# Second feed-forward product by seven products, a second summed buffer, and the order of the last two attention heads

## The chip, the core and the metric

The kernel runs on one core of a Trainium2 chip. A core has a matrix engine (TensorE, PE in the rows), VectorE (DVE), ScalarE (ACT), GpSimd (POOL) and SyncE (SP), which here only starts loads; the instructions of each engine run in the order in which they stand in the program, and engines wait for each other through semaphores. Matmuls read SBUF and add up in PSUM, which has eight banks of 128 x 512 float32. The metric is the device time of one execution in microseconds.

## The reference

One layer over 256 tokens of 2048 features, batch 1. What the change touches:

```
h = rms_norm(x, ffn1_norm);   x = x + 0.5 * swiglu_ffn(h, ffn1_w_in, ffn1_w_out)   # inner width 5632
h = rms_norm(x, mix_norm);    p = h @ w_mix_in            # conv value | conv gate | gMLP u | gMLP v
...                                                        # two mixers, w_mix_out
q = rms_norm(x) @ w_q;  k, v = split(rms_norm(mem) @ w_kv)   # 4 heads of 512, 256 memory tokens
p = softmax(q k^T * 512 ** -0.5);   x = x + (p v) @ w_o
x = x + 0.5 * swiglu_ffn(rms_norm(x, ffn2_norm), ffn2_w_in, ffn2_w_out);   final rms_norm
swiglu_ffn(h, w_in, w_out) = (silu(gate) * up) @ w_out,   gate | up = h @ w_in
```

## The kernel before

**Products.** Every float32 operand is held as two reduced-precision parts, high and low. A weight tile of 128 x 1024 is loaded by SP into a `raw` buffer, ACT casts its high part into an `hl` buffer (1024 columns), DVE subtracts to get the low part, and PE runs three matmuls for each product: high x high, high x low, low x high. One matmul has 128 x 512 outputs.

**First product of a feed-forward (class `FeedForward`).** The 11 groups j write the tiles `h0` to `h10` (128 x 2 x 512, tokens by features). From group 1 on a pair of k tiles is either a plain step (`eight`, 24 matmuls) or a step by seven products instead of eight (`seven`, 21 matmuls), as `PATTERNS` says; the seven products take sums of weight halves, made on DVE, and sums of input halves (`forms`), made once. For three k tiles of each group (`SUMMED`) the low part is not made by DVE: ACT writes minus the high part and the high part, and a load that adds, started by POOL, brings the low part (`summed`). The first feed-forward has two buffers for this from group 1 on (`hl_s` and half of `more`), the second has one (`hl_s`).

**Second product of the first feed-forward.** Four calls of `gemm_n`, one for each 512 output columns: 22 steps of two k tiles, 12 matmuls each (a loaded weight tile holds two k tiles of 512 columns). Its left operand is h turned by PE transposes: 22 turns, each four 128 x 128 transposes of `h` into a bank of the pool `pa` (two banks, tile `aux`), a cast by ACT and a subtraction by DVE into `hA`, `hB`, `hC` or the end of `hl_s`. Four turns stand in the last group of the first product, the other 18 in the first `gemm_n`, one for each step of 12 matmuls. The outputs `o` are copied by ACT, turned in the same way, and joined to x (`joins`), which also writes the left operand `x_hl` of the mixer's products.

**Attention.** For each head: queries, `probabilities` (scores and softmax), `turned` (four transposes of the probabilities into `p_hl`, split of the values into `v_hl`), `attend` (product with the values). For the last two heads the first k tiles of the output product `w_o` are placed between these (`begun`).

**What sets the order.** The code is recorded by a tile framework, whose scheduler orders each engine's instructions; a buffer of a pool is reused when its readers are done.

Of the kernel before, what the change touches and what calls it, by code (L numbers as in the profile page):

```python
# [11 lines left out]
F32 = mybir.dt.float32  # L12
# [5 lines left out]
P = 128  # L18
# [20 lines left out]
SUMMED = ((2, 7, 13), (2, 7, 13))  # L39

# [29 lines left out]
def layer(ctx: ExitStack, tc: tile.TileContext, a: dict):  # L70
# [108 lines left out]
    def gemm_n(w, x_hl, per=0.0, between=None, after=4):  # L179

        acc = [ps.tile([P, 2, 256], F32, name="acc").rearrange("p a b -> p (a b)") for _ in range(2)]
        nk = w.shape[1]
        for k0 in range(0, nk, 2):
# [9 lines left out]
            if between and k0 >= after:  # L193
                between.pop(0)()
# [134 lines left out]
    class FeedForward:  # L329
# [6 lines left out]
        def __init__(self, stack, tags, x_hl, gain, w_in, pattern, summed):  # L336
# [8 lines left out]
            self.h = [(low if j < 8 else high).tile([P, 2, G], F32, name=f"h{j}") for j in range(NG)]  # L345
# [19 lines left out]
            self.first = self.hls[0].rearrange("p a (f two n) -> p (a f) two n", f=2, two=2)  # L365

# [11 lines left out]
        def raw(self, j, k):  # L378
            i = self.raw_at % (4 + len(self.raws))
            self.raw_at += 1  # L380
            raw = wraw.tile([P, 1024], F32, name="raw") if i < 4 else self.raws[i - 4]
            nc.sync.dma_start(out=raw, in_=self.w_in[j, :, k])
            return raw

        def summed(self, at):
# [4 lines left out]
            raw, hl = self.raws_summed[at % len(self.hls)], self.hls[at % len(self.hls)]  # L390
# [21 lines left out]
        def x(self, k, t):  # L412
            s = slice(t * P, (t + 1) * P)
            return self.x_hl[:, k, 0, s], self.x_hl[:, k, 1, s]

        def seven(self, j, p, b, first, last):
# [8 lines left out]
            form = [(self.forms[self.spairs.index(p)][:, f, 0], self.forms[self.spairs.index(p)][:, f, 1]) for f in range(4)]  # L425
            three(b["5"], form[0], w[:, 0, lo], w[:, 1, lo], first, last)
            three(b["7"], form[2], w[:, 0, hi], w[:, 1, hi], first, last)
            nc.vector.tensor_tensor(out=one[:, lo], in0=sums[:, lo], in1=two[:, hi], op=ALU.add)
            w = self.parts(one)
            three(b["6"], form[1], w[:, 0, lo], w[:, 1, lo], first, last)  # L430
            three(b["1"], self.x(k, 0), w[:, 0, hi], w[:, 1, hi], first, last)
            w = self.parts(two)
            three(b["2"], self.x(k + 1, 0), w[:, 0, lo], w[:, 1, lo], first, False)
            three(b["3"], form[3], w[:, 0, hi], w[:, 1, hi], first, False)
            nc.vector.tensor_tensor(out=two[:, lo], in0=two[:, lo], in1=one[:, lo], op=ALU.subtract)
            w = self.parts(two, G)
            three(b["4"], self.x(k + 1, 1), w[:, 0, lo], w[:, 1, lo], first, False)
# [5 lines left out]
        def eight(self, j, p, b, first, last, plain):  # L443
            for k in (2 * p, 2 * p + 1):
                at = (j, k) in self.sums_at and self.sums_at.index((j, k))
                w = self.parts(self.raw(j, k), last=plain) if at is False else self.hls[at % len(self.hls)]
                begin = [(1, 1)] if first and k % 2 == 0 else []
                acc = [[b["2"], b["3"]], [b["4"], b["8"]]]
                by_two(acc, self.x_hl[:, k], w[:, 0], w[:, 1], k, begin, last and k % 2 == 1)
# [3 lines left out]
                self.next = None if at is False else at + len(self.hls)  # L453
# [9 lines left out]

        def group(self, j, r, after=()):
            b = {}
            for name in "57":
                b[name] = bank(ps if name == "5" else pa, "acc" if name == "5" else "aux")
            b["6"] = bank(pa, "aux")
            for name in "1234":
                b[name] = bank(ps, "acc")  # L470
            b["8"] = bank(ps, "acc")
# [3 lines left out]
            for p, c in enumerate(self.pattern):  # L475
                if c == "S":
                    self.seven(j, p, b, p == 0, p == self.spairs[-1])
# [730 lines left out]
```

## Time and profile before

| | us |
|---|---|
| median of 3 runs (lowest, highest) | 2100.37 (2097.94, 2103.01) |
| the profiled execution | 2096.62 |
| its span, first to last instruction | 2094.9 |
| PE busy | 2082.5 |
| DVE busy | 1577.4 |
| ACT busy | 1165.2 |

The table is read so: the span is the time of the profiled execution from its first instruction to its last, 1.7 us less than its device time. Busy PE is not PE at its peak, because matmuls overlap: a matmul of 512 columns is listed with 0.39 us, and the next starts 0.23 us later. So a wait of PE is seen in the distance of two starts, and a wait under about 0.16 us does not show as idle time.

### The profile page before, as it was taken

Reading aid. Unit: us, or ns where it says so; the run is one execution under the profiler, and the core shown is the slowest. Engines: PE = TensorE matmul, PEld = TensorE weight load, DVE = VectorE, ACT = ScalarE, POOL = GpSimd, SP = SyncE. Lnnn points to the kernel's source line nnn. Section 1 sums busy time; section 2 is a strip of 40 time slices with the busy share of each in tenths; the row PEclk is TensorE's granted clock in tenths of the full one; section 3 lists DMA queues with packets and bytes.
Section 4 is the critical chain, followed back from the end, with each engine's and each line's share of the span. In section 5 each row is a group of like instructions: output and inputs, shape, how many; then the busy total and the mean of one; then the engine's idle time right before and its main releaser. Section 6 shows DMA issues by size and latency. Waiting matters only on the chain.

```text
span 2094.9 us, 26646 instructions
## 1 busy us (share of the span) xinstructions
PE 2082.5 (99%) x9786; PEld 1741.6 (83%) x9786; DVE 1577.4 (75%) x2217; ACT 1165.2 (56%) x1451; POOL 67.7 (3%) x83
## 2 busy tenths in 40 slices
PE   9999999999999999999999999999999999999998
PEld 7888888888888888888888898888888888888886
DVE  7888888875655589888877666778888888787754
ACT  8665666554544454445665454556665666554443
POOL 0000000000000000000000000000000000000000
PEclk9999999999999999999999999999999999999999
DMA  9787778755665666555555543576777777556664
GB/s 368 241 263 246 226 228 263 228 183 169 226 189 188 216 233 198 187 180 183 182 197 188 186 157 117 200 272 218 217 248 251 241 225 246 182 163 203 195 192 152
DMA packets 122387, 442.34 MB, mean 211 GB/s; under 512 B 13584, under 2 KB 13968, under 8 KB 121872
## 3 DMA queue, kind: packets, MB, share of 16 engines
q1 hardware_dynamic: 113040, 407.08, 57.0%
q0 software_dynamic: 8640, 32.51, 8.3%
q8 instruction: 76, 1.25, 0.2%
q10 hardware_dynamic: 576, 1.06, 0.1%
q14 instruction: 55, 0.45, 0.1%
HBM read 438.49 MB, written 2.10 MB: 210 GB/s over the span
## 4 chain that ended last, share of the span: by engine, by line
PE 96%; DMA 2%; issue 1%; ACT 1%; DVE 0%; POOL 0%; SPq 0%; DVEq 0%; ACTq 0%; POOLq 0%
PE acc L192 12%; PE acc L191 12%; PE acc L190 12%; PE acc L319 9%; PE acc L321 9%; PE acc L318 9%; PE acc L144 8%; PE acc L151 4%; PE acc L307 3%; PE acc L305 3%; PE acc L306 3%; PE aux L293 1%; PE aux L307 1%; PE aux L305 1%; PE aux L306 1%
## 5 line engine op out<-in xcount | busy, mean ns | idle before, releaser
L116 DVE TENSOR_TENSOR hl<-raw,hl 128x1024 fp32r<-128x1024 f32 (+1 forms) x402 | 488.5, 1216 | 277.3 <-ACT hl L115 276.3
L115 ACT CAST hl<-raw 128x1024 fp32r<-128x1024 f32 (+1 forms) x402 | 419.6, 1045 | 477.8 <-PE acc L192 291.0
L373 DVE TENSOR_TENSOR hl<-spare,hl 128x1024 fp32r<-128x1024 f32 (+1 forms) x128 | 146.6, 1149 | 34.0 <-ACT hl L372 31.0
L372 ACT CAST hl<-spare 128x1024 fp32r<-128x1024 f32 (+1 forms) x128 | 126.2, 994 | 69.4 <-PE acc L321 25.9
L319 PE MATMUL acc<-hl,x_hl 128*128 128x512 f32 x408 | 147.7, 391 | 0.3 <-DVE hl L124 0.2
L373 DVE TENSOR_TENSOR hl<-raw,hl 128x1024 fp32r<-128x1024 f32 (+1 forms) x107 | 120.7, 1131 | 29.7 <-ACT hl L372 28.3
L372 ACT CAST hl<-raw 128x1024 fp32r<-128x1024 f32 (+1 forms) x107 | 103.5, 979 | 69.6 <-PE acc L321 26.7
L318 PE MATMUL acc<-hl,x_hl 128*128 128x512 f32 x408 | 141.8, 390 | 0.3 <-ACT hl L123 0.3
L321 PE MATMUL acc<-hl,x_hl 128*128 128x512 f32 x408 | 126.5, 389 | 0.0
L372 ACT CAST ring<-spare 128x1024 fp32r<-128x1024 f32 (+1 forms) x81 | 80.4, 997 | 58.9 <-PE acc L321 19.0
L373 DVE TENSOR_TENSOR ring<-spare,ring 128x1024 fp32r<-128x1024 f32 (+1 forms) x81 | 93.0, 1153 | 13.9 <-ACT ring L372 12.6
L191 PE MATMUL acc<-hl,m_hl 128*128 128x512 f32 x256 | 100.3, 392 | 0.0
L191 PE MATMUL acc<-hl,x_hl 128*128 128x512 f32 x256 | 100.3, 392 | 0.0
L192 PE MATMUL acc<-hl,m_hl 128*128 128x512 f32 x256 | 100.2, 391 | 0.0
L192 PE MATMUL acc<-hl,x_hl 128*128 128x512 f32 x256 | 99.8, 390 | 0.0
L319 PE MATMUL acc<-ring,x_hl 128*128 128x512 f32 x248 | 91.4, 389 | 0.0
L190 PE MATMUL acc<-hl,m_hl 128*128 128x512 f32 x256 | 91.2, 392 | 0.0
L318 PEld LDWEIGHTS acc<-hl,x_hl 128*128 128x128 f32 x408 | 76.4, 188 | 16.6 <-ACT hl L123 0.5
L319 PEld LDWEIGHTS acc<-hl,x_hl 128*128 128x128 f32 x408 | 76.2, 188 | 16.8 <-DVE hl L373 0.8
L190 PE MATMUL acc<-hl,x_hl 128*128 128x512 f32 x256 | 90.0, 391 | 0.0
L321 PEld LDWEIGHTS acc<-hl,x_hl 128*128 128x128 f32 x408 | 76.6, 188 | 16.0
L318 PE MATMUL acc<-ring,x_hl 128*128 128x512 f32 x248 | 88.8, 389 | 0.0
(362 smaller groups left out, 4974.9 us busy)
## 6 DMA issues: line engine op xcount, KB each, us to landing
spare<-in_ffn_w_in SPq DMA_DIRECT2D x195, 512.0 KB, 7.0
raw<-in_ffn_w_out SPq DMA_DIRECT2D x176, 512.0 KB, 3.5
raw<-in_ffn_w_in SPq DMA_DIRECT2D x156, 512.0 KB, 6.4
hl_s<-in_ffn_w_in POOLq DMA_DIRECT2D x44, 512.0 KB, 8.8
raw<-in_w_mix_vg SPq DMA_DIRECT2D x32, 512.0 KB, 4.5
raw<-in_w_k SPq DMA_DIRECT2D x32, 512.0 KB, 3.6
raw<-in_w_v SPq DMA_DIRECT2D x32, 512.0 KB, 4.3
raw<-in_w_mix_out SPq DMA_DIRECT2D x32, 512.0 KB, 4.6
```

The costliest lines, as they stand in the source:

```text
L115: nc.scalar.copy(out=hl[:, 0, :size], in_=raw[:, :size])
L116: newest[0] = nc.vector.tensor_tensor(out=hl[:, 1, :size], in0=raw[:, :size], in1=hl[:, 0, :size].bitcast(F32), op=ALU.subtract)
L144: nc.tensor.matmul(acc, lhsT=hi[:, k], rhs=xs[k], start=first and k == 0, stop=last and k == kk - 1, skip_group_check=True,)
L151: nc.tensor.matmul(acc[:, 0], lhsT=lo[:, k], rhs=xs[k][:, 0], start=False, stop=last and k == kk - 1, skip_group_check=True,)
L190: nc.tensor.matmul(acc[t], lhsT=x[:, 0, s], rhs=hi[:, k], start=k0 + k == 0, stop=False)
L191: nc.tensor.matmul(acc[t], lhsT=x[:, 0, s], rhs=lo[:, k], start=False, stop=False)
L192: nc.tensor.matmul(acc[t], lhsT=x[:, 1, s], rhs=hi[:, k], start=False, stop=k0 + k == nk - 1)
L318: nc.tensor.matmul(acc[t][g], lhsT=x[:, 0, s], rhs=hi[:, cols[g]], start=(t, g) in first, stop=False)
L319: nc.tensor.matmul(acc[t][g], lhsT=x[:, 0, s], rhs=lo[:, cols[g]], start=False, stop=False)
L321: nc.tensor.matmul(acc[t][g], lhsT=x[:, 1, s], rhs=hi[:, cols[g]], start=False, stop=last)
L372: self.cast = nc.scalar.copy(out=hl[:, 0, :n], in_=raw[:, :n])
L373: newest[0] = nc.vector.tensor_tensor(out=hl[:, 1, :n], in0=raw[:, :n], in1=hl[:, 0, :n].bitcast(F32), op=ALU.subtract)
```

## The change

It does four things.

1. The second product of the first feed-forward is computed in two blocks of 1024 output columns (`out_block`) instead of four of 512. Of the 22 pairs of k tiles four (9, 12, 15 and 18) are steps by seven. The 18 turns come faster, two or three to a pair, and the turns with numbers 9, 12, 15 and 18 also make the sums of input halves (`out_sides`). Two more `raw` buffers (`raw_out0`, `raw_out1`) and the buffer of weight sums lie where `h4` to `h6` were, two more `hl` buffers and the sums in `more_out`.
2. The first product of the mixer (`w_mix_vg`) runs its first two column groups in halves: k tiles 0 to 7 of both, then 8 to 15 of both.
3. The second feed-forward gets a second summed buffer (`hl_s2`) for the groups up to 7; `h9` and `h10` take its place later, and `h8` is its `raw` buffer until group 8 writes it.
4. In attention's last two heads the first part of `w_o` tile 1 is loaded in two halves around the turn of head 2, and the turn of head 3 is recorded before, not after, four k tiles of `w_o` tile 0.

The core of the diff:

```diff
+OUT_S = (9, 12, 15, 18)
+OUT_STEPS = (
+    list(range(KF // 2)),
+    [9, 0, 1, 12, 2, 3, 15, 4, 5, 18, 6, 7, 8, 10, 11, 13, 14, 16, 17, 19, 20, 21],
+)
...
+            if pair:
+                second = high.tile([P, 2, 1024], F32R, name="hl_s2", tag="pair")
+                self.h += [high.tile([P, 2, G], F32, name="h8"), None, None]
...
+        def buffer(self, at):
+            return at % 2 if not self.pair or self.sums_at[at][0] < 8 else 0
...
+        def out_sides(self, form, tp):
+            f1, f2 = ev.tile([P, T], F32, name="tu"), ev.tile([P, T], F32, name="tg")
+            second = ev.tile([P, T], F32, name="sq")
+            nc.scalar.copy(out=second.rearrange("p (k t) -> p k t", k=2), in_=tp[:, :, P:])
...
+            nc.vector.scalar_tensor_tensor(out=f[0], in0=a21, scalar=-1.0, in1=a22, op0=ALU.mult, op1=ALU.subtract)
+            nc.vector.scalar_tensor_tensor(out=f[1], in0=f[0], scalar=-1.0, in1=a11, op0=ALU.mult, op1=ALU.subtract)
+            nc.vector.tensor_tensor(out=f[2], in0=a11, in1=a21, op=ALU.subtract)
+            nc.vector.tensor_tensor(out=f[3], in0=a12, in1=f[1], op=ALU.subtract)
...
-        for n in range(4):
-            acc = gemm_n(a["ffn1_w_out"][n], ff.of, per=0.8 if n else 0.0, between=turns, after=0 if n == 0 else 4)
...
+        def turns_first(i):
...
+            for _ in range(2 if i < 4 else 1):
+                next_turn()
+            if i == 6:
+                stack.enter_context(ff.late)
+                ff.high.close()
+                pool = rest["pool"] = stack.enter_context(tc.tile_pool(name="ffn1", bufs=1, reuse_waits="tile"))
+                ff.sums = pool.tile([P, 1024], F32, name="sums_out")
+                ff.raws += [pool.tile([P, 1024], F32, name=f"raw_out{q}") for q in range(2)]
...
+        o = ff.out_block(0, result, turns_first, next_turn)
...
             begun(0, 0, 8)
-            begun(1, 0, 8)
+            begun(1, 0, 4)
             turn_now(2)()
+            begun(1, 4, 4)
             state["p"] = probabilities(3, q_next)
             attend(2, *state["v"])
             begun(2, 0, 8)
+            turn_now(3)()
             begun(0, 8, 4)
-            turn_now(3)()
             begun(1, 8, 4)
...
-        ff = FeedForward(stack, ("S0", "S1", "S2"), x_hl, lambda k: col("ffn2_norm", k), a["ffn2_w_in"], PATTERNS[1], SUMMED[1])
+        ff = FeedForward(stack, ("S0", "S1", "S2"), x_hl, lambda k: col("ffn2_norm", k), a["ffn2_w_in"], PATTERNS[1], SUMMED[1], pair=True)
```

How instructions move at three places. In the rows, a name's number tells buffers apart, and line numbers of the changed program are some 8 to 150 higher.

**Place 1, the last turns of h in the second product.** PE before, at the second turn of `h8` and the first of `h9` (`aux` is a turn's bank, `hl` a cast weight tile):

```order
L190 MATMUL acc_3485<-hl_3854,hB_3647 128x512
L191 MATMUL acc_3484<-hl_3854,hB_3647 128x512
L191 MATMUL acc_3485<-hl_3854,hB_3647 128x512
L293 MATMUL aux_3816<-ident_81,h8_128 128x128 x4
L293 MATMUL aux_3845<-ident_81,h9_129 128x128 x4
L192 MATMUL acc_3484<-hl_3854,hB_3647 128x512
L192 MATMUL acc_3485<-hl_3854,hB_3647 128x512
```

PE now, at all turns of `h8`, `h9` and `h10`:

```order
L329 MATMUL acc_3486<-hl_3879,hA_3455 128x512
L301 MATMUL aux_3759<-ident_81,h8_128 128x128 x4
L301 MATMUL aux_3783<-ident_81,h8_128 128x128 x4
L301 MATMUL aux_3812<-ident_81,h9_129 128x128 x4
L301 MATMUL aux_3847<-ident_81,h9_129 128x128 x4
L301 MATMUL aux_3870<-ident_81,h10_130 128x128 x4
L301 MATMUL aux_3894<-ident_81,h10_130 128x128 x4
L326 MATMUL acc_3483<-hl_3909,hA_3455 128x512
```

Before, two turns stand together and 24 matmuls lie between such pairs; now six turns stand in a row, without a matmul between them. The turn before them, the second of `h7` (`aux_3723`), stands five matmuls ahead of the first row above.

ACT before, in the same stretch (L115 casts a weight tile, L123 a turn; now L392 and L131):

```order
L123 CAST hB_3647<-aux_3768 128x2x256
L123 CAST hB_3647<-aux_3792 128x2x256
L115 CAST hl_3878<-raw_3876 128x1024
L115 CAST hl_3902<-raw_3900 128x1024
L123 CAST hB_3647<-aux_3816 128x2x256
L123 CAST hC_3844<-aux_3845 128x2x256
```

ACT now, from the second turn of `h8` to the weight tile that PE multiplies next:

```order
L131 CAST hB_3626<-aux_3783 128x2x256
L131 CAST hC_3811<-aux_3812 128x2x256
L574 COPY sq_3821<-aux_3812 128x256
L131 CAST hC_3811<-aux_3847 128x2x256
L131 CAST more_out_3528<-tu_3819 128x2x128
L131 CAST more_out_3528<-tg_3820 128x2x128
L131 CAST hC_3811<-aux_3870 128x2x256
L131 CAST hC_3811<-aux_3894 128x2x256
L392 CAST hl_3909<-raw_out1_3907 128x1024
L392 CAST hl_3926<-raw_3924 128x1024
```

Before, casts of weight tiles stood between the casts of turns; now the cast of the next weight tile, `hl_3909`, stands behind the casts of all six turns, and `out_sides` (lines 574 and on) stands among them.

**Place 2, the turn of the probabilities of head 2.** PE before (`e` the probabilities, `p_hl` turned, `v_hl` the values):

```order
L151 MATMUL acc_10144<-o_hl_9122,hl_10169 128x256 x8
L969 MATMUL aux_10189<-ident_81,e_10114 128x128
L969 MATMUL aux_10194<-ident_81,e_10114 128x128
L969 MATMUL aux_10189<-ident_81,e_10135 128x128
L969 MATMUL aux_10194<-ident_81,e_10135 128x128
L129 MATMUL acc_10247<-p_hl_10188,v_hl_10199 128x256
```

PE now:

```order
L159 MATMUL acc_10212<-o_hl_9190,hl_10264 128x256 x4
L1107 MATMUL aux_10249<-ident_81,e_10182 128x128
L1107 MATMUL aux_10254<-ident_81,e_10182 128x128
L1107 MATMUL aux_10249<-ident_81,e_10203 128x128
L1107 MATMUL aux_10254<-ident_81,e_10203 128x128
L137 MATMUL acc_10320<-p_hl_10248,v_hl_10259 128x256
```

The product that reads `p_hl` stands right behind the four transposes in both; only the weight loads ahead of them are cut otherwise.

**Place 3, ACT at the end of attention.** Before, behind the last casts of head 3 (`o_hl`):

```order
L123 CAST o_hl_9122<-acc_10384 128x256
L115 CAST hl_10457<-raw_10455 128x512
L115 CAST hl_10477<-raw_10475 128x1024
L115 CAST hl_10506<-raw_10504 128x1024
L268 ACTIVATE x_hl_10415<-xT_3478,pv_82 128x256
```

ACT now:

```order
L131 CAST o_hl_9190<-acc_10457 128x256
L123 CAST hl_10530<-raw_10528 128x512
L421 ACTIVATE hl_s2_11194<-h8_11195 128x1024
L422 CAST hl_s2_11194<-h8_11195 128x1024
L123 CAST hl_10550<-raw_10548 128x1024
L123 CAST hl_10579<-raw_10577 128x1024
```

The two instructions that fill the second summed buffer now stand ahead of the cast of a `w_o` tile.

## Rows read from the trace of the kernel before

**Rows 1.** The page: busy time by engine, and the chain that ended last

```profile
PE 2082.5 (99%) x9786; PEld 1741.6 (83%) x9786; DVE 1577.4 (75%) x2217; ACT 1165.2 (56%) x1451; POOL 67.7 (3%) x83
PE 96%; DMA 2%; issue 1%; ACT 1%; DVE 0%; POOL 0%; SPq 0%; DVEq 0%; ACTq 0%; POOLq 0%
```

**Rows 2.** PE's waits: line, what it waited for, total us, times, longest

```profile
PE acc L319 <- DMA hl_s<-in_ffn_w_in: 0.9, 1, 0.9
PE acc L129 <- ACT p_hl L123: 0.6, 1, 0.6
PE acc L129 <- DVE o_hl L124: 0.3, 1, 0.3
```

**Rows 3.** Chain in order of time: start, us, matmuls of 512, 128 and 256 columns

```profile
106.86 0.91 PE acc L318 x4
...
489.66 0.87 PE aux L293 x8
...
1099.60 1.91 PE acc L151 x16
```

**Rows 4.** Busy time by engine: second product of the first feed-forward, groups of the second

```profile
448.00:690.00 242.00, 242.00 (x1124) 200.57 (x1124) 141.88 (x167) 121.21 (x158) 0.00 (x0) 1.00 0.60 194
...
1600.00:1700.00 100.00, 100.00 (x443) 82.81 (x442) 83.12 (x99) 63.02 (x68) 6.11 (x7) 1.00 0.79 248
```

**Rows 5.** Timeline: start, us, engine, line; two turns in a row

```profile
489.50 1.03 PE L293 MATMUL aux<-ident,h 128*128 128x128 f32 x8
...
490.14 0.59 ACT L123 CAST hA<-aux 128x512 fp32r<-128x512 f32 x1 [0.29 <-PE aux L293]
...
490.62 0.59 ACT L123 CAST hB<-aux 128x512 fp32r<-128x512 f32 x1
...
491.02 0.68 DVE L124 TENSOR_TENSOR hA<-aux,hA 128x512 fp32r<-128x512 f32 x1
...
491.62 0.68 DVE L124 TENSOR_TENSOR hB<-aux,hB 128x512 fp32r<-128x512 f32 x1
```

**Rows 6.** Timeline: a turn's cast and the subtraction that waits for it alone

```profile
478.73 0.59 ACT L123 CAST hA<-aux 128x512 fp32r<-128x512 f32 x1 [1.19 <-PE aux L293]
...
479.35 0.69 DVE L124 TENSOR_TENSOR hA<-aux,hA 128x512 fp32r<-128x512 f32 x1 [0.44 <-ACT hA L123]
```

**Rows 7.** Groups: busy us, mean ns of one, idle before; operations like the added ones

```profile
L405 DVE SCALAR_TENSOR_TENSOR spare<-spare 128x128 f32<-128x128 f32 x3 | 0.9, 291 | 0.1
...
L726 ACT COPY pad<-aux 128x256 f32<-128x256 f32 x2 | 0.6, 376 | 0.3 <-PE aux L293 0.3
...
L115 ACT CAST hl<-raw 128x1024 fp32r<-128x1024 f32 x105 | 110.3, 1052 | 130.0 <-PE acc L192 107.1 <-DMA raw<-in_ffn_w_out 10.0 <-PE acc L321 4.6
...
L116 DVE TENSOR_TENSOR hl<-raw,hl 128x1024 fp32r<-128x1024 f32 x104 | 127.2, 1224 | 115.6 <-ACT hl L115 115.5
```

**Rows 8.** DMA issues: KB each, median us from issue to landing

```profile
raw<-in_ffn_w_out SPq DMA_DIRECT2D x176, 512.0 KB, 3.5
raw<-in_ffn_w_in SPq DMA_DIRECT2D x156, 512.0 KB, 6.4
...
raw<-in_w_o SPq DMA_DIRECT2D x29, 512.0 KB, 4.6
```

**Rows 9.** Groups: the first of the two casts that fill a summed buffer

```profile
L392 ACT ACTIVATE hl_s<-spare 128x1024 fp32r<-128x1024 f32 x14 | 14.9, 1064 | 20.1 <-PE acc L319 20.1
```

**Rows 10.** Timeline of PE: around the wait for the summed buffer

```profile
1506.44 0.39 PE L318 MATMUL acc<-hl_s,x_hl 128*128 128x512 f32 x1
1507.77 0.73 PE L319 MATMUL acc<-hl_s,x_hl 128*128 128x512 f32 x2 [0.94 <-DMA hl_s<-in_ffn_w_in]
```

**Rows 11.** Clock (the third number from the end) at the program's end, and PE at its start

```profile
2086.00:2088.00 2.00, 0.05 (x1) 0.00 (x0) 1.21 (x3) 1.97 (x4) 0.06 (x1) 1.00 0.31 129
...
2089.00:2090.00 1.00, 0.00 (x0) 0.00 (x0) 1.00 (x3) 0.85 (x2) 0.20 (x1) 0.71 0.88 356
...
1.06 4.05 PE L219 MATMUL aux<-ones 128*128 128x128 f32 x22 [1.06 <-DVE ones L216]
```

More of the change, by code (lines that the diff above doesn't have):

```diff
@@ L192, in gemm_n @@
                     nc.tensor.matmul(acc[t], lhsT=x[:, 1, s], rhs=hi[:, k], start=False, stop=k0 + k == nk - 1)
-            if between and k0 >= after:
+            if between and k0 >= after and k0 % step == 0:
                 between.pop(0)()
@@ L441, in seven, with eight @@
                 self.next = None
-        def eight(self, j, p, b, first, last, plain):
+        def eight(self, j, p, b, last, plain, between=None):
             for k in (2 * p, 2 * p + 1):
+                if between is not None and k % 2 == 1:
+                    between()
                 at = (j, k) in self.sums_at and self.sums_at.index((j, k))
[L446 to L449, printed above, removed]
+                w = self.parts(self.raw(j, k), last=plain) if at is False else self.hls[self.buffer(at)]
+                names = [["2", "3"], ["4", "8"]]
+                begin = [(t, g) for t in range(2) for g in range(2) if self.begins(names[t][g])]
+                acc = [[b[name] for name in row] for row in names]
+                by_two(acc, self.x(j, k), w[:, 0], w[:, 1], k, begin, last and k % 2 == 1)
                 if self.next is not None:
@@ L462, in give, with banks, joins_sevens @@
                 )
+        def banks(self, b, names):
+            for name in names:
+                b[name] = bank(pa if name in "67" else ps, "aux" if name in "67" else "acc")
+        def joins_sevens(self, b, p1, u2, u4, u5):
+            nc.scalar.copy(out=p1, in_=b["1"])
+            nc.vector.tensor_tensor(out=u2, in0=p1, in1=b["6"], op=ALU.add)
+            nc.vector.tensor_tensor(out=u4, in0=u2, in1=b["5"], op=ALU.add)
+            nc.vector.tensor_tensor(out=u2, in0=u2, in1=b["7"], op=ALU.add)
+            nc.vector.tensor_tensor(out=u5, in0=u2, in1=b["5"], op=ALU.add)
         def group(self, j, r, after=()):
+            if self.pair and j == NG - 2:
+                both = self.high_pool.tile([P, 2, 2, G], F32, name="h_pair", tag="pair")
+                self.h[NG - 2:] = [both[:, i] for i in range(2)]
             b = {}
[L466 to L471, printed above, removed]
+            self.begun = set()
+            self.banks(b, "57612348")
             after = list(after)
@@ new lines, in result, with turned, beside_second @@
+        def result():
+            return rest["pool"].tile([P, 2, 2 * G], F32, name="o", bufs=2)
+        def turned(o, n):
+            return [turning(o, 2 * i * P, joins(8 * n + 2 * i)) for i in range(4)]
+        o = ff.out_block(0, result, turns_first, next_turn)
+        turns += turned(o, 0)
+        def beside_second(i):
+            if i == OUT_STEPS[1].index(OUT_S[-1]):
+                ff.ring = []
+                rest["x_hl"] = gained_tile("S2")
+            elif i > 9:
+                beside(1.4)
+                if i % 2 == 0 and turns:
+                    turns.pop(0)()
@@ L655, in layer @@
+        o = ff.out_block(1, result, beside_second)
+        turns += turned(o, 1)
+        x_hl = rest["x_hl"]
         finish()
```

140 lines of the change are left out of this document (100 added, 40 removed).

## The prediction

> **What bounds the kernel now.** I read the page first. PE is busy for 99% of the span and 96% of the chain that ended last lies on it [rows 1], so what counts is how many matmuls there are and where PE stands still. The view of waits gives PE only three entries worth naming, together under 2 us: one for the summed buffer in the second feed-forward, two for the turned probabilities and outputs in attention [rows 2]. So there is little waiting to remove; the large term can only be fewer matmuls, and the large risk a new wait. The chain in order of time gives the pitch at which PE runs: four 512-column matmuls in 0.91 us (0.2275 each), eight 128-column transposes in 0.87 (0.109 each), sixteen 256-column matmuls in 1.91 (0.119 each) [rows 3]. Then the place of the change, by engine: over the second product (448 to 690) PE is busy throughout, DVE 142 of 242 us, ACT 121; in a stretch of feed-forward groups that already hold steps by seven, DVE is busy 83 of 100 us and PE still all 100 [rows 4]. So sevens alone, with an even supply, are covered there.
>
> **The change part by part.** The sum is made against the profiled execution, 2096.6 us, which is 3.8 below the median 2100.37; I add those 3.8 back at the end.
>
> A. *Fewer matmuls.* Four steps by seven in each of two blocks save three matmuls each of 512 columns: 24 x 0.2275 = **-5.46 us**. All of PE's time is on the path, so this is a gain to the full.
>
> B. *Six turns in a row, with ACT's next weight cast behind them.* This is the term that decides. Before, PE's order had 24 matmuls between pairs of turns; now the six turns of h8 to h10 stand together, and only two `aux` banks exist. A turn can start only when the subtraction of the turn two back has released its bank. From the timeline of two turns in a row: the cast starts 0.64 after the transposes, lasts 0.59, the next starts 0.48 later; subtractions take 0.68, 0.60 apart [rows 5]; alone, cast start to subtraction start is 0.62 [rows 6]. `out_sides` at the turns 15 (h7's second) and 18 (h9's first) adds an ACT copy of 0.38 from the same bank and four small DVE operations of 0.29, three of which read the bank [rows 7]; I take 0.21 between their starts, by the 0.08 by which rows 5's spacing of subtractions is under their duration. Let t = 0 be when PE starts h8's first turn. h7's second turn began 0.43 + 5 x 0.2275 = 1.57 earlier.
> - Its subtraction ends near 0.38, the copy at 0.80, the three small operations and the subtraction of h8's first turn (cast 0.64 to 1.23) share DVE until about 2.25. h8's second turn, ready at 0.43, starts near 2.3: idle 1.85.
> - h9's first turn follows, to 3.17. The cast of h8's second runs 2.94 to 3.53, its subtraction ends 4.25; h9's second starts 4.3: idle 1.1.
> - h9's first is subtracted by 4.85, copied by 5.27, the cast of h9's second ends 5.75; small operations and its subtraction end near 6.65; h10's first starts 6.7: idle 2.0. h10's second follows to 7.57.
> - Their casts end near 8.4, and only then comes the cast of `hl_3909`, 1.05 [rows 7]: PE restarts at 9.4, idle 1.9, and after four matmuls with the high part (0.91) waits 0.4 more for the low part (1.22 on DVE [rows 7]).
>
> Sum 1.85 + 1.1 + 2.0 + 1.9 + 0.4 = **+7.25 us**. The load of `raw_out1` starts about 0.5 us before t = 0; a load of this weight lands 3.5 us after its issue, of the first product 6.4 [rows 8], before ACT's turn at 8.4, so nothing is added for it. The unknown is whether the copy and the small operations of one bank run beside each other and beside the subtraction. If so, 0.7 goes at each of the two places: 5.85. If each hand-over is slower by 0.2 at the nine of the chain, 9. I take 7.25, because the order has each read of a bank wait for the one before it.
>
> The Trainium skill (PSUM — Partial Sum Buffer, "PSUM bank collisions raise a hardware error") says that two engines must not touch one bank in the same cycle, reads too, and that accesses have to be guarded by bank. By it the copy can't run beside the subtraction, and the term is 7.25 and not 5.85; no run here shows it yet.
>
> C. *ACT at the end of attention.* The two casts that fill `hl_s2` now stand ahead of a `w_o` tile. From the end of head 3's product with the values, which frees the place of `h8` for its load, PE has 20 matmuls of 512 columns and 20 of 256 until it needs `hl_10550`: 20 x 0.2275 + 20 x 0.119 = 6.93. ACT needs the load (4.6 for a `w_o` tile in the same stretch [rows 8]), twice 1.06 [rows 9] and 1.05: 7.8. **+0.8 us**; with a load of 3.5, nothing, with one of 6.4, 2.7 [rows 8].
>
> D. *Second summed buffer.* The one wait it aims at is at 1506: starts 1.33 apart where 0.2275 is the pitch, so 1.1, listed with 0.94 [rows 10]; later, smaller ones bring it to 1.6. For the groups up to 7 two buffers end it. From group 8 on there is one buffer again, and the switch from two to one puts one load behind a full turn of that buffer, as at 1506. I take **0**: 1.6 gone, and as much back; -1.6 if the switch is covered, +0.5 if it costs more than the old one.
>
> E. *Attention.* The waits for `p_hl` (0.6) and `o_hl` (0.3) [rows 2] stand where the product follows the four transposes at once. It still does, in both heads; what moves is the loads ahead of it. **0**; -1.6 if all gaps around both go, +0.5 if the second half load comes late.
>
> F. *The mixer's first product in halves.* The same matmuls in another order; four turns of o at its start stand in the room of two: **0**, covered by the 48 matmuls of each half (10.9 us). Without that cover, one turn's chain of 1.9 us (0.64 + 0.59 + 0.68 [rows 5]).
>
> G. *DVE and ACT work of the steps by seven.* About 48 us more of DVE in the second product, 142 to 190 of some 237: 80%, under the 83% of the stretch where PE did not wait [rows 4]. **0** while weight tiles are cast ahead; the rival below prices it.
>
> Sum: -5.46 + 7.25 + 0.8 + 0 = +2.6. Profiled 2096.6 + 2.6 = 2099.2, and with 3.8 to the median: **2103.0 us**.
>
> **The rivals.**
>
> *R1, the gain as meant.* PE does not wait at the six turns because bank and casts run further ahead than I add up, and the old waits go: -5.46 - 1.6, less some residue of 0.2: 2100.4 - 6.9 = 2093.5. For it: a chain of this kind is covered in the kernel before, and DVE has room. Against it: in the order nothing else is left for PE between those turns, so the chain can't be covered by matmuls.
>
> *R2, the clock falls in the gap, and the time ends on the slower side.* The 9.4 us from t = 0 hold only 24 transposes, 2.6 us of work. At the program's end, PE's last matmul ends at 2086; the granted clock is still 1.00 until 2088 and 0.71 in 2089 to 2090 [rows 11], so idling alone brings it down from 2.4 GHz, and before the end of the gap it could be at 1.2. At the program's start 22 passes of 128 columns took 4.05 us, where 22 x 0.109 = 2.4 and 0.16 of overhang would be the full rate: 1.5 lost [rows 11]. Price: that 1.5, plus up to four turns of the chain at half rate, 4 x 0.43 = 1.7; in the middle 2.3, so 2105.3. It decides if PE's transposes do not keep the clock up: no single idle stretch in the sum is longer than 2.0 us, which the rows at the end show to be survived.
>
> The Trainium skill (TensorE: Matmul & The Clock Gate, "Part 4: PE-mode transpose") says that transposes don't count as busy for the clock in the way that matmuls do; by it the whole 9.4 us would count as a pause, and R2 is right. No stretch of the trace before holds transposes alone, so none shows it.
>
> *R3, DVE becomes the bound in the steps by seven.* Such a step takes about 6.4 us on DVE (three full subtractions and a half one at 1.22 and 0.68, three sums of halves) against 21 x 0.2275 = 4.8 on PE. In block 1 the four stand among plain steps, in block 0 behind the six turns, where buffers are empty. It decides if the buffers ahead run out; 1.6 at each of the eight, and with half of them exposed +6.4: 2109.4. Against it: rows 4's stretch of the same steps.
>
> **How the numbers follow.** This kernel's measurements can tell about 0.2%, 4.2 us: faster is under 2096.2, slower over 2104.6. Forecast 0.58, R1 0.12, R2 0.22, R3 0.08. The forecast's own ends are -5.46 + 5.85 + 0 - 1.6 - 1.6 = -2.8 (2097.6) and -5.46 + 9 + 2.7 + 0.5 + 0.5 = +7.2 (2107.6). Of it 0.49 lies within the bound, 0.07 above, 0.02 below; R2 0.07 within, 0.15 above; R1 below and R3 above. So faster 0.14, same 0.56, slower 0.30. The range 2096.5 to 2107.5 leaves out R1, most of R3 and a little of the forecast's ends: 0.2.
>
> **What would show it.** In the changed kernel PE's timeline should have six groups of four transposes with idle stretches of 1 to 2 us between, ended by DVE's release of `aux`, and about 9.4 us from the first to the next matmul (A and B); PE's instructions 24 fewer in the long form. The granted clock of that stretch decides R2. At attention's end a wait for ACT's cast of a `w_o` tile of under 1 us shows C; a wait for `hl_s` in group 8 or 9 shows D. I am wrong if the six turns pass in under 5 us, if `hl_3909`'s cast does not wait for them, or if PE waits in the steps by seven for DVE.

## The result, and the profile after

| | kernel before | changed kernel |
|---|---|---|
| median of 22 runs, us | 2099.32 | 2102.15 |
| ratio to the kernel before, 95% interval | | 1.0013 (1.0007 to 1.0018) |
| the profiled execution, us | 2096.62 | 2102.46 |
| its span, us | 2094.9 | 2100.7 |
| matmuls on PE | 9786 | 9762 |

The changed kernel is slower by 0.13%, 2.8 us, inside the 0.2% that the prediction called no change; the forecast was 2103.0 us, 2.6 us above the kernel before. One profiled execution is not the median: the kernel before lies 2.7 us under it, the changed one 0.3 above it, so the spans differ by 5.8 where the medians differ by 2.8.

The page of the changed kernel, busy time and chain, to be read against [rows 1]:

```profile
PE 2080.8 (99%) x9762; PEld 1739.6 (83%) x9762; DVE 1624.7 (77%) x2306; ACT 1180.0 (56%) x1474; POOL 67.7 (3%) x83
...
PE 84%; issue 11%; DMA 2%; ACT 1%; POOL 1%; DVE 1%; DVEq 0%; POOLq 0%; ACTq 0%; SPq 0%
```

PE has 24 matmuls fewer and is busy 1.7 us less, and still the span is longer. PE's waits (line, what it waited for, total us, times, longest), which answer to [rows 2]:

```profile
PE aux L301 <- DVE hB L132: 2.6, 2, 1.6
PE acc L326 <- ACT hl L392: 2.1, 2, 1.6
PE aux L301 <- DVE hC L132: 1.8, 1, 1.8
PE acc L152 <- ACT hl L123: 1.4, 1, 1.4
...
PE acc L327 <- DMA hl_s<-in_ffn_w_in: 0.7, 1, 0.7
PE acc L137 <- ACT p_hl L131: 0.6, 1, 0.6
PE acc L137 <- DVE o_hl L132: 0.3, 1, 0.3
```

The first three are new and belong to the six turns in a row (L301 is a turn, L392 casts a weight tile; of the second row's 2.1 us, 1.6 stand there and 0.5 at the program's start), the fourth is new at the end of attention, the last three stood in [rows 2] too. The timeline of PE at the six turns (start, us, line, operation, and in brackets the idle time before it and what ended it):

```profile
511.12 0.60 PE L301 MATMUL aux<-ident,h 128*128 128x128 f32 x4
513.37 1.09 PE L301 MATMUL aux<-ident,h 128*128 128x128 f32 x8 [1.65 <-DVE hB L132]
515.42 0.66 PE L301 MATMUL aux<-ident,h 128*128 128x128 f32 x4 [0.96 <-DVE hB L132]
517.87 1.97 PE L301 MATMUL aux<-ident,h 128*128 128x128 f32 x8 [1.79 <-DVE hC L132]
521.46 2.08 PE L326 MATMUL acc<-hl,hA 128*128 128x512 f32 x4 [1.62 <-ACT hl L392]
523.34 1.05 PE L327 MATMUL acc<-hl,hA 128*128 128x512 f32 x2
```

Counted from start to start against the pitch, PE stands still for 1.81, 1.13, 1.96 and 1.93 us, and loses 0.37 between the first two of the four matmuls: 7.20 together. From the first turn (511.12) to the next matmul (521.46) it takes 10.3 us. And the eight transposes at 517.87 take 1.97 us where the eight at 513.37 took 1.09. The windows of the same stretch tell why (the third number from the end is the granted clock):

```profile
513.00:516.00 3.00, 1.67 (x12) 1.27 (x12) 2.55 (x6) 1.48 (x3) 0.00 (x0) 0.99 0.93 371
516.00:518.00 2.00, 0.20 (x2) 0.13 (x2) 1.56 (x6) 1.26 (x3) 0.00 (x0) 0.50 0.06 25
...
524.00:526.00 2.00, 2.00 (x6) 1.52 (x6) 2.00 (x3) 0.35 (x1) 0.00 (x0) 0.50 0.85 260
526.00:528.00 2.00, 2.00 (x10) 1.68 (x9) 0.31 (x2) 1.05 (x1) 0.00 (x0) 0.95 0.62 227
```

The clock is at half, 1.2 of 2.4 GHz, from 516 to about 526. It costs 0.85 us at the transposes and 1.9 at the 16 matmuls behind them (5.95 us where the pitch makes 3.64, less the 0.37 above): 2.75. This is the second of the prediction's rivals, on top of the forecast and not in place of it.

ACT and DVE between the turns show the chain from which the 7.25 us were added up. First rows of ACT, then of DVE, from the timeline around h8's second turn and h9's first (L574 is the copy of `out_sides`, L577 to L579 are small operations of it, L132 a subtraction, L131 a turn's cast):

```profile
514.06 0.59 ACT L131 CAST hB<-aux 128x512 fp32r<-128x512 f32 x1
514.54 0.59 ACT L131 CAST hC<-aux 128x512 fp32r<-128x512 f32 x1
516.00 0.37 ACT L574 COPY sq<-aux 128x256 f32<-128x256 f32 x1 [0.87 <-DVE hC L132]
```

The same stretch on DVE:

```profile
515.29 0.68 DVE L132 TENSOR_TENSOR hC<-aux,hC 128x512 fp32r<-128x512 f32 x1
516.41 0.29 DVE L577 SCALAR_TENSOR_TENSOR tu<-sq 128x128 f32<-128x128 f32 x1 [0.44 <-ACT sq L574]
516.73 0.29 DVE L578 SCALAR_TENSOR_TENSOR tu<-tu,aux 128x128 f32<-128x128 f32 x1
516.94 0.28 DVE L579 TENSOR_TENSOR tg<-aux,sq 128x128 f32<-128x128 f32 x1
517.14 0.68 DVE L132 TENSOR_TENSOR hC<-aux,hC 128x512 fp32r<-128x512 f32 x1
```

The copy starts at 516.00, 0.03 after the subtraction from the same bank has ended (515.97), and the small operations follow the copy. In these rows none of the two engines' reads of one bank overlap, as the prediction took it. What would happen if they did, this order can't show; it never lets them.

At the end of attention, the issue of the load of `h8` (SPq is SP's queue), then ACT between head 3's last casts and the `w_o` tile:

```profile
1303.84 0.33 SPq L420 DMA_DIRECT2D h<-in_ffn_w_in  x1
...
1307.03 0.62 ACT L123 CAST hl<-raw 128x512 fp32r<-128x512 f32 x1 [2.86 <-PE acc L159]
1309.12 1.06 ACT L421 ACTIVATE hl_s<-h 128x1024 fp32r<-128x1024 f32 x1 [1.47 <-DMA h<-in_ffn_w_in]
1310.09 1.03 ACT L422 CAST hl_s<-h 128x1024 fp32r<-128x1024 f32 x1
1311.02 1.99 ACT L123 CAST hl<-raw 128x1024 fp32r<-128x1024 f32 x2
```

The load of `h8` takes from 1303.84 to 1309.1, some 5.3 us. ACT waits 1.47 us for it, then fills `hl_s2`, and only then casts the tile that PE waits for until 1312.11: 1.54 us more than the pitch.

### The profile page after: what moved, and what is told of

Same layout as the page of the kernel before. It is cut to its first block, busy times and chain, and to the rows that moved or that the text cites. A ratio compares the mean times of both kernels' runs of the same rounds, so it can differ in the third digit from the quotient of the medians.

```text
span 2100.7 us, 26741 instructions
## 1 busy us (share of the span) xinstructions
PE 2080.8 (99%) x9762; PEld 1739.6 (83%) x9762; DVE 1624.7 (77%) x2306; ACT 1180.0 (56%) x1474; POOL 67.7 (3%) x83
## 4 chain that ended last, share of the span: by engine, by line
PE 84%; issue 11%; DMA 2%; ACT 1%; POOL 1%; DVE 1%; DVEq 0%; POOLq 0%; ACTq 0%; SPq 0%
PE acc L327 10%; PE acc L326 10%; PE acc L329 10%; PE acc L199 8%; PE acc L200 8%; PE acc L198 8%; PE acc L152 8%; PE acc L159 4%; PE acc L313 3%; PE acc L315 3%; PE acc L314 3%; PE aux L301 1%; PE aux L314 1%; PE aux L315 1%; PE aux L313 1%
## 5 line engine op out<-in xcount | busy, mean ns | idle before, releaser
L123 ACT CAST hl<-raw 128x1024 fp32r<-128x1024 f32 (+1 forms) x315 | 327.4, 1040 | 354.1 <-PE acc L200 197.0
L124 DVE TENSOR_TENSOR hl<-raw,hl 128x1024 fp32r<-128x1024 f32 (+1 forms) x315 | 380.6, 1210 | 166.1 <-ACT hl L123 164.7
L393 DVE TENSOR_TENSOR hl<-raw,hl 128x1024 fp32r<-128x1024 f32 (+1 forms) x156 | 178.8, 1149 | 55.8 <-ACT hl L392 54.6
L392 ACT CAST hl<-raw 128x1024 fp32r<-128x1024 f32 (+1 forms) x156 | 153.5, 994 | 114.9 <-PE acc L329 52.9
L392 ACT CAST hl<-spare 128x1024 fp32r<-128x1024 f32 (+1 forms) x128 | 126.3, 994 | 72.1 <-PE acc L329 31.9
L392 ACT CAST ring<-spare 128x1024 fp32r<-128x1024 f32 (+1 forms) x81 | 80.4, 998 | 57.8 <-PE acc L329 19.3
```

The lines of the kernel that those rows point to most:

```text
L123: nc.scalar.copy(out=hl[:, 0, :size], in_=raw[:, :size])
L124: newest[0] = nc.vector.tensor_tensor(out=hl[:, 1, :size], in0=raw[:, :size], in1=hl[:, 0, :size].bitcast(F32), op=ALU.subtract)
L392: self.cast = nc.scalar.copy(out=hl[:, 0, :n], in_=raw[:, :n])
L393: newest[0] = nc.vector.tensor_tensor(out=hl[:, 1, :n], in0=raw[:, :n], in1=hl[:, 0, :n].bitcast(F32), op=ALU.subtract)
```

## The experiments

All were run beside the kernel before, five rounds each (three for the kernel before itself). Medians of one chip are set against each other only.

| run | median, us | ratio to the kernel before (95%) |
|---|---|---|
| changed kernel again | 2102.36 | 1.0014 (1.0005 to 1.0023) |
| spread | 2095.60 | 0.9980 (0.9971 to 0.9989) |
| fill | 2099.98 | 0.9999 (0.9990 to 1.0008) |
| late | 2100.23 | 1.0003 (0.9994 to 1.0012) |
| best | 2090.09 | 0.9956 (0.9943 to 0.9969) |
| no_pair | 2102.83 | 1.0015 (1.0007 to 1.0024) |
| sides | 2099.53 | 1.0001 (0.9993 to 1.0010) |
| kernel before again | 2099.95 | 1.0001 (0.9992 to 1.0010) |
| best again | 2089.63 | 0.9956 (0.9944 to 0.9969) |
| two_sevens | 2092.05 | 0.9965 (0.9951 to 0.9978) |
| no_attn_vg | 2103.14 | 1.0019 (1.0010 to 1.0028) |

The first four shared one chip, the next four another, the last three a third.

**The changed kernel again.**

> The changed kernel, nothing edited, beside the kernel before on one chip. If the six turns and the slow clock behind them are fixed costs of the order, the profile repeats: idle stretches of 1.8, 1.1, 2.0 and 1.9 us at the turns of h8 to h10, granted clock 0.50 until about 526, span 2100 to 2102 us, time 1.0007 to 1.0018 of the kernel before. If the first profile was an unlucky execution, the clock stays at 1.00 there and the span is 2.7 us less.

The idle times repeat to 0.1 us (1.82, 1.13, 1.96, 1.84, 0.37). The clock doesn't. The windows of this execution:

```profile
518.00:520.00 2.00, 0.34 (x4) 0.10 (x1) 2.00 (x5) 2.00 (x4) 0.00 (x0) 0.89 0.00 0
520.00:522.00 2.00, 1.99 (x5) 1.61 (x6) 2.00 (x4) 1.05 (x2) 0.00 (x0) 0.50 0.01 4
522.00:524.00 2.00, 2.00 (x8) 1.60 (x7) 2.00 (x3) 0.90 (x1) 0.00 (x0) 0.76 0.79 262
```

It fell near 519.6, 3.6 us later than in the first profile and one pause later in the row of turns, was coming back in 522 to 524, spared the transposes and cost about 1.2 us instead of 2.75. Neither expectation holds as it was put: the fall is no accident of one execution, and its price is not fixed either. The timed runs say the same: the mean granted clock was 0.996 to 0.998 in all 33 of the changed kernel, and 0.998 or 0.999 in the 32 of the kernel before that stood beside the last 11.

**fill: keep PE busy in the gaps.** 26 matmuls that nobody reads, behind the turns 16, 18, 19 and 21, into a bank that is free there.

```diff
...
+                    with tc.issue_after(turned_last[0].ins):
+                        for _ in range({16: 7, 18: 4, 19: 8, 21: 7}.get(i, 0)):
+                            nc.tensor.matmul(self.fill, lhsT=x[:, :P], rhs=x[:, :G], start=True, stop=True)
```

> The changed kernel with 26 further matmuls of 512 columns into a free PSUM bank, which nobody reads, behind the turns of h8 to h10: 7, 4, 8 and 7 of them, 5.9 us at the full pitch, in idle stretches of 6.8 us together. They add work to TensorE and take away no wait. If idle time of TensorE brings the clock down there, the clock stays at 1.00, the transposes behind run at 0.11 and the matmuls at 0.23 us, and the time falls by 2.7 us against the changed kernel although it does more: 2099.4 us, 1.0000 of the kernel before. If the clock falls for another reason, nothing changes: 2102.2 us; if the added matmuls delay the turns, up to 1 us more.

PE does 5.9 us more work and the kernel is 2.4 us faster than the changed kernel on the same chip (2099.98 against 2102.36). PE's timeline (L671 are the added matmuls, L303 the turns):

```profile
511.64 1.87 PE L671 MATMUL acc<-hl_s 128*128 128x512 f32 x7
...
518.05 1.09 PE L303 MATMUL aux<-ident,h 128*128 128x128 f32 x8
518.90 1.84 PE L671 MATMUL acc<-hl_s 128*128 128x512 f32 x7
520.82 1.20 PE L328 MATMUL acc<-hl,hA 128*128 128x512 f32 x4
```

The windows of the same stretch, with the granted clock third from the end:

```profile
516.00:518.00 2.00, 2.00 (x11) 1.41 (x9) 1.53 (x6) 1.27 (x3) 0.00 (x0) 1.00 0.05 18
518.00:520.00 2.00, 2.00 (x14) 1.78 (x14) 1.86 (x5) 1.66 (x4) 0.00 (x0) 1.00 0.00 0
```

The transposes at 518.05 take 1.09 again, four matmuls 1.20 instead of 2.08, and the clock stays at 1.00. The granted clock of its 11 timed runs was 0.998 or 0.999, as in the kernel before. The chain of turns is as long as it was: the next weight's matmuls start 9.5 us after h8's first turn, where the prediction had 9.4. So the two parts of the loss are separate: the chain holds PE for some 7 us, and the pauses in PE's work bring the clock down.

**sides: shorten the chain.** The sums of halves read the high part in SBUF and not the turn's bank.

```diff
-                        self.out_sides(self.out_forms[OUT_S.index(i)], tp)
+                        self.out_sides(self.out_forms[OUT_S.index(i)], d[:, :, 0].bitcast(F32))
```

> The changed kernel, in which the sums of input halves are made from the high part in SBUF and not from the turn's PSUM bank (the low part of the inputs is left out of these sums); as many instructions. If the copy and the three small operations that must read the bank one after the other lengthen the six-turn chain by what the trace shows (about 1 us at each of two places), the idle time at the turns falls from 6.8 to about 4.9 and the time by 2.0 us: 2100.2, 1.0004 of the kernel before, and up to 1.5 more if the clock then falls later. If the wait of the next weight tile's cast behind the six turns is all that counts, the idle time moves to that tile and the time stays within 0.5 us of the changed kernel's.

PE at the last turns:

```profile
513.30 0.66 PE L301 MATMUL aux<-ident,h 128*128 128x128 f32 x4 [0.97 <-DVE hB L132]
514.24 0.66 PE L301 MATMUL aux<-ident,h 128*128 128x128 f32 x4 [0.28 <-DVE hC L132]
515.57 0.66 PE L301 MATMUL aux<-ident,h 128*128 128x128 f32 x4 [0.68 <-DVE hC L132]
518.15 2.07 PE L326 MATMUL acc<-hl,hA 128*128 128x512 f32 x4 [1.93 <-ACT hl L392]
```

From start to start idle time fell to 1.13 + 0.44 + 0.84 + 2.09 + 0.37 = 4.87 us, the 4.9 expected; by the ratios, 1.0001 against 1.0013, the time is 2.5 us under the changed kernel's, with an interval of 0.0009 to either side of the first. But the edit moved an instruction too: h8's first turn now stands ahead of seven matmuls, and the first idle stretch, 1.81 us, is gone whole. What the bank did there and what the order did can't be told apart. Where PE's order is the same, at the turns of h9 and h10, idle time fell from 1.96 to 0.44 + 0.84 = 1.28: 0.7 us for the copy and the small operations, the price that the prediction gave for one place. The last stretch, for the weight's cast behind all turns, stays, and the clock still fell, near 517.8.

**spread: take the pile apart.** Two turns for each pair instead of three at first, and the buffers over `h4` to `h6` opened four pairs later.

```diff
-OUT_S = (9, 12, 15, 18)
+OUT_S = (11, 13, 15, 18)
...
-            for _ in range(2 if i < 4 else 1):
-                next_turn()
-            if i == 6:
+            next_turn()
+            if i == 10:
```

> Same change, but the turns of h come two for each pair of k tiles instead of three, the buffers over h4 to h6 are opened four pairs later, and the first steps by seven are the pairs 11 and 13 instead of 9 and 12; as many steps by seven, as many matmuls. If the six turns in a row cost what the two traces say (7.2 us of idle time and some 2.7 us at the low clock), the time falls by 9.9 us against the changed kernel: 2092.3 us, 0.9966 of the kernel before, and the stretch from 500 to 530 runs at clock 1.00 without a wait over 0.3 us. If the work of the turns must be waited for wherever it stands (VectorE is the bound of the second product), the waits return in the steps by seven, and the time stays within 2099 to 2102 us.

It gained 6.8 us against the changed kernel, not 9.9. From 500 to 550 PE now waits for nothing and the clock stays at 1.00, but a new wait stands at 573, in the timeline of PE:

```profile
571.17 0.39 PE L329 MATMUL acc<-more_out,hB 128*128 128x512 f32 x1
573.08 0.50 PE L313 MATMUL acc<-more_out 128*128 128x512 f32 x1 [1.52 <-ACT more_out L392]
```

Ahead of it the issue of the second load of the sum, then DVE with its waits for the two loads:

```profile
564.04 0.33 SPq L403 DMA_DIRECT2D raw_out<-in_ffn_w_out  x1
...
564.23 0.69 DVE L460 TENSOR_TENSOR sums_out<-raw 128x512 f32<-128x512 f32 x1 [0.21 <-DMA raw<-in_ffn_w_out]
571.18 0.69 DVE L461 TENSOR_TENSOR sums_out<-raw_out,raw 128x512 f32<-128x512 f32 x1 [6.26 <-DMA raw_out<-in_ffn_w_out]
```

And the window behind it, the granted clock third from the end:

```profile
574.00:577.00 3.00, 2.97 (x7) 2.39 (x8) 3.00 (x4) 1.91 (x3) 0.00 (x0) 0.52 0.01 3
```

The pairs 11, 13 and 15 stand too close: DVE waits 6.3 us for a load into `raw_out`, whose buffer the step before had held until 564.0. The load is issued at once, and takes until 571.1, 7 us where the median of these loads is 4.3. PE then stands still for 1.7 us, and the clock falls behind it: about 2.1 us more. Neither theory had this: it is the buffer that comes free late, and a slow load into it, and not DVE's work, that runs out first.

**best: all waits that the change brought or left.** Turns at the even pace of *spread* and steps by seven at every third pair, the first filling of `hl_s2` behind group 0's last cast, and, in both heads, four k tiles of `w_o` held behind the four transposes.

```diff
-OUT_S = (9, 12, 15, 18)
+OUT_S = (11, 14, 17, 20)
...
+                with tc.issue_after(self.cast.ins):
+                    self.summed(1)
...
+            with tc.issue_after(turned_last[0].ins):
+                begun(1, 4, 4)
...
+            with tc.issue_after(turned_last[0].ins):
+                begun(0, 8, 4)
...
```

> All that the change does, with the three waits that it brought or left taken away: the turns two for each pair of k tiles and the steps by seven at the pairs 11, 14, 17 and 20 (in the run called spread the pairs 11, 13 and 15 stood too close: a load into raw_out1 took from 564 to 571 us, TensorE waited 1.7 us for the sum of it and lost 2.1 us more at the low clock); the first filling of hl_s2 behind group 0's last cast; and in attention four k tiles of w_o held behind the four transposes of the probabilities, so that the product that reads them does not follow at once. Against the changed kernel: 9.9 for the turns and the clock, 1.6 for hl_s2, 1.5 for attention: 2102.2 - 13.0 = 2089.2 us, 0.9951 of the kernel before. If VectorE bounds the steps by seven at this spacing too, one or two waits of 1 to 2 us with 1 to 2 us at the low clock behind each return between 530 and 600: 2092 to 2096 us.

2090.09 us, 0.9956: 0.44% faster than the kernel before, and the same ratio again in a second set. By the ratios that is 12.2 us under the changed kernel, where 13.0 were expected. PE's waits in its profile, all that the view lists:

```profile
PE aux L227 <- DVE ones L224: 1.1, 1, 1.1
PE acc L327 <- DMA hl_s<-in_ffn_w_in: 0.9, 1, 0.9
```

The windows of the first block's steps by seven, and of the whole second product:

```profile
530.00:600.00 70.00, 70.00 (x312) 57.97 (x311) 58.77 (x67) 37.30 (x40) 0.00 (x0) 1.00 0.56 188
467.20:712.00 244.80, 244.80 (x1127) 203.16 (x1126) 183.28 (x241) 134.16 (x177) 0.00 (x0) 1.00 0.60 198
```

PE is busy without a break, the clock full, and DVE busy for 59 of 70 us among the steps by seven without PE waiting for it. The waits at the turned probabilities are gone as well; the edit in attention was not run alone, so its share of the 12.2 us rests on these waits (0.75 and 0.49 us) and not on a time. And not all of the distance to the kernel before is accounted for: the matmuls saved (5.5 us) and these two waits make 6.7, the profiled executions lie 7.2 apart (2089.41 and 2096.62), and the ratio makes it 9.2. The rest belongs to the open question of the last run below.

**late: the first filling alone.** Only the second of the three edits above.

> The changed kernel with the first filling of the second summed buffer (hl_s2) recorded behind the last cast of the second feed-forward's group 0, so that ScalarE does not do its two casts ahead of a w_o tile at the end of attention. If those two casts are what TensorE waits 1.65 us for at 1312, this wait is gone and the time falls by 1.6 us against the changed kernel: 2100.5 us, 1.0006 of the kernel before. If the load of that buffer comes too late then, a wait of 1 us or more comes back at the first summed tile of group 1, around 1450 us, and nothing is won.

2.1 us under the changed kernel on the same chip; ACT casts the `w_o` tile at 1308.3 and the wait of 1.54 us is gone. The wait for the summed buffer grew in this execution to 1.5 at 1719 and 0.7 at 1762, where the changed kernel's two profiles had 0.9 and nothing, and 0.6 and 0.15. It moves from execution to execution, so no more is read from it than its size.

**no_pair: the second summed buffer undone.**

```diff
         def buffer(self, at):
+            if self.pair is None:
+                return 0
...
-        ff = FeedForward(stack, ("S0", "S1", "S2"), x_hl, lambda k: col("ffn2_norm", k), a["ffn2_w_in"], PATTERNS[1], SUMMED[1], pair=True)
+        ff = FeedForward(stack, ("S0", "S1", "S2"), x_hl, lambda k: col("ffn2_norm", k), a["ffn2_w_in"], PATTERNS[1], SUMMED[1], pair=None)
```

> The changed kernel with the second feed-forward's second summed buffer undone (one buffer, as before). If the sums of both profiles hold, the wait of 1.65 us for a w_o tile goes, the wait at 1720 (1.0 us) goes, and the wait of the kernel before at group 3 (1.5 us) returns: 1.1 us less than the changed kernel, 2101.0 us, 1.0008 of the kernel before. If the second buffer were worth what it was made for, the time would be 1 us longer than the changed kernel's: 2103.2.

1.0015: the time of the changed kernel. The wait for the `w_o` tile is gone, and the one buffer's waits are back, larger than in the kernel before (PE's waits):

```profile
PE acc L327 <- DMA hl_s<-in_ffn_w_in: 2.0, 3, 1.0
```

From start to start they are 0.8, 1.1 and 0.5. So by these waits what the second buffer gains in the second feed-forward is about what its first filling costs in attention, and the two can be had apart (*late*). The time, between the two that were expected, can't decide between them: the interval is 1.8 us to either side.

**two_sevens: the matmuls saved, alone.** The kernel called best, with the steps by seven only at the pairs 14 and 20.

```diff
-OUT_S = (11, 14, 17, 20)
+OUT_S = (14, 20)
...
```

> The kernel of the run called best with only two steps by seven in each block of the second product (pairs 14 and 20), two plain steps in the place of the other two: 12 matmuls of 512 columns more. If the matmuls saved are a gain to the full and VectorE's further work is covered, it is 12 x 0.2275 = 2.7 us longer than best: 2092.8 us, 0.9969 of the kernel before. If VectorE's work eats half of the gain, 1.4 us longer or less.

2.4 us longer than best beside it on the chip (2092.05 against 2089.63), with 2.7 expected for 12 matmuls. The two intervals overlap, and the times alone don't rule out the 1.4 of the other theory. The second product does, from its first matmul to its last:

```profile
467.30:715.00 247.70, 247.70 (x1140) 205.32 (x1138) 164.84 (x205) 126.57 (x163) 0.00 (x0) 1.00 0.59 195
```

It takes 247.7 us where *best* takes 244.8 in both of its profiles, at full clock and without a wait: 2.9 us for the 12 matmuls.

**no_attn_vg: two parts undone.** Attention's order and the halves of the mixer's first product as they were.

> The changed kernel with two of its parts undone: the order of attention's last two heads and the mixer's first product in halves. If both are worth nothing, as their traces say (the waits of 0.75 and 0.49 us at the turned probabilities stand unchanged), the time is that of the changed kernel: 2102.2 us, 1.0013 of the kernel before, with the same waits. If the halves hide the last turns of the product before, 1 to 2 us are lost: 2103 to 2104, with a wait between 675 and 720.

1.0019 beside 1.0013 and 1.0014 for the changed kernel: no difference that these intervals, 1.9 us to either side here, can tell. The waits at the turned probabilities are 0.75 and 0.49 us in the kernel before, in the changed one and here. A wait of 0.6 us at 753, which the changed kernel does not have, is what its profile shows that the halves could be worth; the kernel before had 0.5 near there in one of two executions.

**The kernel before again.**

> The kernel before, nothing edited. Its profiled execution of 2096.6 us lies 2.7 below the median of its 22 runs, that of the changed kernel at its median. If that was chance, this profile has a span of 2096 to 2099 us, with 1 to 3 us lost at places where the first one lost nothing (the clock at the start, the wait for the summed buffer); ratio 1.0000. If the profiler takes the kernel before 2.7 us faster than the timed runs do, the span is 2095 again.

Its profiled execution took 2097.5 us, its median is 2099.95: again 2.4 under. Places differ (0.4 at 37, 0.5 at 743, the summed buffer at 1675 and not at 1507), sums hardly. Over all kernels here a profiled execution lay between 2.7 below and 1.7 above the median of its timed runs; why the kernel before sits at the lower end both times stays open.

## Why the prediction was right, point by point

- **A, fewer matmuls, -5.46.** 24 matmuls fewer in the profile; *two_sevens* gives 2.4 for the half of them by the medians and 2.9 by the length of the second product, where 2.7 is due. Shown, with PE on the path throughout.
- **B, six turns in a row, +7.25.** The four idle stretches are 1.81, 1.13, 1.96 and 1.93 where 1.85, 1.1, 2.0 and 1.9 were worked out. The last 0.4 is right by luck: it was to be a wait behind the four matmuls for the low part, but at the low clock these last so long that the low part is there first (DVE ends it at 522.67, PE goes on at 523.34); the 0.37 lies between the first two of the four. At full clock, in *fill*, a wait of 0.23 does stand behind the four. *spread* and *best* take the pile away and the time falls; *sides* shows 0.7 us for the bank at one of the two places. That none of the bank's readers run beside each other was the right end of the range.
- **The rival R2, the clock.** It had a chance of 0.22, and its mechanism happened, though not its time of 2105.3: 2.75 us in one profile, 1.2 in the next, 2.3 forecast. *fill* shows that the cause is what PE does in the pause: with the gaps filled, and the same chain, the clock stays. The step that failed is the sentence that no single idle stretch is longer than what the rows at the program's end survive: [rows 11] show one pause at the end, not four pauses with transposes between, and the clock fell at the start of the third of them in the first profile, in the fourth in the second. The rule of the Trainium skill named there (TensorE: Matmul & The Clock Gate, "Part 4: PE-mode transpose") says that transposes don't count as busy in the way that matmuls do. The trace is in keeping with it, with 24 transposes in 10.3 us and the clock at 0.50 for its second half, but it doesn't show it: PE also stood idle for 6.8 of these us, and no run parts the two.
- **C, ACT at the end of attention, +0.8.** Right place, mis-sized: 1.54 us (1.3 to 1.8 in the other profiles with this order). The term that was too small is the load of `h8`: 5.3 us from issue to landing where 4.6 were taken. *late* removes the wait.
- **D, the second summed buffer, 0.** 1.5 to 1.6 us of waits were to go and as much to come back at group 8. They went at 1507 and 1549, and 0.9 came at 1720; in other executions these waits add up to 0.7 to 2.2 with two buffers, 0.8 to 2.5 with one. *no_pair* shows no effect of C and D together beyond its interval of 1.8 us.
- **E, F, G, all 0.** The waits in attention stand to the hundredth of a microsecond, so E is shown. For F *no_attn_vg* leaves room for the 0.6 us of one wait. For G, DVE was busy for 184 of the 254.6 us of the second product (467.5 to 722.1), 72%, where 190 of 237 was taken; in *best* it was 183 of 244.8, 75%. Against the 142 before that is 42 more, 48 forecast, and PE did not wait for it in the steps by seven.
- **R3, DVE as the bound in the steps by seven.** Not in the changed kernel, nor in *best*; a wait in a step by seven came in *spread*, from a load and not from DVE's work.

So the direction and each large term hold, and the total is nearer than the terms deserve. By the first profiles the changed kernel was 5.8 us longer, 3.2 more than forecast: 2.75 from the clock, 0.7 from C, less what D gave. By the second ones (2100.18 and 2097.53) it was 2.7 longer. The medians differ by 2.8, because the kernel before's profiled execution was 2.7 us under its median and the changed kernel's was not; I had added the offset of 3.8 from three runs to both. Against the interval 1.0007 to 1.0018, 1.5 to 3.8 us, the 2.6 forecast stands in the middle by luck: the clock and C were left out or too small, and about as much is hidden in the timed runs of the kernel before, which take 2.4 to 2.7 us more than its profiled executions for a reason that no run shows.

## What to carry to other kernels

A gain in matmuls can be lost when the steps that prepare its operands pile up at one place of the order: read the order for runs of small operations through a pool of two, and for a cast, needed by the next product, that is queued behind them. Price such a pile twice, once as a chain of hand-overs and once more for the clock behind it. Then spread the pile: here the same saving at an even pace turned 0.13% slower into 0.20% faster (*spread*), and into 0.44% faster with the steps by seven further apart and the other waits removed (*best*).

## What the runs showed of the hardware

The clock's fall was not in the prediction's main case, and its price depends on when it comes and how long it lasts. In the changed kernel it fell near 516 in one execution and near 520 in the next, in the same row of turns, and cost 2.75 and 1.2 us. It fell there in each of the six profiles in which these turns stand close and nothing fills the pauses (the changed kernel's two, *late*, *no_pair*, *no_attn_vg*, *sides*), between 515.6 and 519.6, and stayed at 0.50 for 3.4 to 10.2 us; in *fill*, *spread* and *best* it did not fall there. One pause of 1.7 us in *spread* was followed by 0.52 over 574 to 577, although PE had been busy without a break before it; a pause of 1.5 us at 1312 in the changed kernel was followed by a clock of 1.00, as the window behind it shows:

```profile
1312.00:1316.00 4.00, 3.89 (x18) 3.24 (x19) 3.91 (x6) 4.00 (x9) 0.00 (x0) 1.00 0.97 206
```

What sets the one apart from the other was not tried. Filling the pauses with matmuls that nobody needs kept the clock at 1.00 and made the kernel 2.4 us faster with 5.9 us more work.
